# Row scale of a norm as a diagonal in the products that turn x, block inverses' last copies on ScalarE, and other places for the late modulation

## The chip, the cores and the metric

The kernel runs on one core of one Trainium2 chip. The metric is the device time of one execution in microseconds (us). The engines are named as the profile names them: PE is TensorE (PEld its weight loads), DVE is VectorE, ACT is ScalarE, SP is the engine whose queue issues nearly all DMAs. SBUF is the memory on the chip, PSUM the accumulators that PE writes, in banks of 128 rows by 512 f32.

## What is computed

One block of three sublayers on x of 256 rows (tokens) by 2048 columns, all in float32. Each sublayer has the same frame around its inner function:

```python
def sandwich_sublayer(x, fn, gain_pre, gain_post, shift, scale, gate, weight):
    h = modulate(rms_norm(x, gain_pre), shift, scale)   # h*(1+scale)+shift
    y = rms_norm(fn(h), gain_post)
    return x + weight * (1 + gate[:, None, :]) * y
```

The inner functions are a SwiGLU of width 5632 (`(silu(h @ w_gate) * (h @ w_up)) @ w_down`), a mixer, and a second SwiGLU. The mixer multiplies h by w_in (2048 x 5472), sends 512 columns through causal averages over 2, 4, 8 and 16 rows and four 128 x 128 products, and 24 heads of 64 through an RWKV-7 recurrence, and multiplies the joined result by w_out (2048 x 2048). Shift, scale and gate of the three sublayers, nine vectors of 2048, come from one product, `silu(c) @ w_ada + b_ada`, with a w_ada of 2048 x 18432 for a single row c. This product is called the modulation below; its vectors are numbered 0 to 8, and 6 and 7 are shift and scale of the third sublayer.

## The kernel before, in words

**Arithmetic.** A weight is loaded as f32 (`load`, L173, 1 MB as a rule, tile raw), and split into a rounded part hi (ACT, L185) and the rest lo (DVE, L186). The activations stand in hT, with the 2048 columns on the partitions in 16 blocks of 128, again as a high and a low part. Each product is three matmuls, hi with high, hi with low, lo with high (L201 and the wide form, L212 and L213).

**Norm and turn (`pre_begin` L389, `pre_rows` L399, `pre_block` L404).** The scale of a row is computed from the sum of its squares (`pre_begin`, or `post_rows` for the second and third sublayer). `pre_rows` multiplies x by it on ACT and writes y (L402). `pre_block` takes blocks of columns, in sizes of 2, 2, 4, 4 and 4: PE transposes y, 128 x 128 at a time, two columns by two halves of the rows into one bank (L417); ACT copies a column's 256 rows to the high part of hT with the norm's gain and the modulation (L421), copies it once more in full (L425; in the first block of the second and third sublayer column 1 is done on DVE instead, L423), and DVE subtracts for the low part (L426).

**Outer stage (`outer`, L631).** The first products of each sublayer run block by block behind these turned blocks. In an FFN the blocks of 2 and 2 are merged for most of the loads; the first block has two loads, and the merged second one ten. At fixed loads a `tick` runs one step of the modulation.

**Modulation.** `ada_step` (L259) does a quarter of the 2048 rows of w_ada for up to 1024 columns: DMAs into ada tiles (four in an FFN, two in the mixer), a multiply-add on DVE for each (L255, L257), and after four steps a product with ones on PE that sums over the partitions (`ada_mod`, L311) and an add of b_ada (L323). In the mixer the generator `ada_run` (L273) does the same through four places in x, which is copied out to memory meanwhile (L878) and back (L954); three loads run ahead of the sums. `ADA_AHEAD` lets it go as far as the third of the five blocks of vectors 6 and 7. The other two blocks are made in FFN2's outer stage, four steps beside the merged block (`TICKS2`, loads 3, 5, 7, 9) and four beside the next.

**The mixer's stages (`stage`, L882).** After its outer stage the mixer runs seven stages of 12 slots. Six have a part `rwkv_a` of the next pair of heads, with `rwkv_b` of the one before, and two pieces of weight products in each slot (w_in's, in the sixth also w_out's). The last has `rwkv_b` alone and three pieces in two slots. In here PE's order is fixed by hand (`self.ordered`): every matmul depends on the one listed before it. DVE's modulation sums are held behind the last operation marked urgent (`later`, `mark`). `rwkv_b` inverts lower triangular blocks in PSUM and SBUF by quarters: slot 4 multiplies into bank pb and copies it to pm, half on ACT (L1254), half on DVE (L1255), slot 5 multiplies pm with Z1 into bank zb and copies it into X, half on ACT (L1260), half on DVE (L1261), whose other entries DVE has filled by a mask (L1246). L1089 holds products of a decay tile with a constant triangle, plain f32 of 128 x 128, four in each of the six groups; L1118 uses bank ga in slot 4 of `rwkv_a`, L1234 copies At.

**w_out.** Two of its four column blocks are gathered in the stages (`out_piece`, L913), the other two run afterwards (L973, `rows_block` L596), the third in banks pb and zb, the fourth in sb, y and mm. Behind each column block follow statistics and z = y times gain (`post_rows`, L469), and behind the fourth the row scales and the update of x, which lead over to FFN2 (L541 to L557). L907 and L908 cast the finished rows of the recurrence into hT; the last of these wait for the recurrence's end.

The order on every engine and in SP's queue is laid out when the program is built, by priorities in the order of the code and a model of durations, within these dependences.

## Time and profile before

| | |
|---|---|
| median of 3 runs | 2139.73 us (2135.27 to 2146.23) |
| profiled execution | 2141.48 us |
| its span | 2139.7 us |
| mean granted clock of PE | 0.982 |

The span goes from the first to the last instruction in the profile. Its stages, read from the timeline (us from the start of the span):

| stretch | what runs |
|---|---|
| 0 to 27 | loads of x, first modulation, first row scales |
| 27 to 230 | FFN1's outer stage |
| 230 to 803 | rest of FFN1 |
| 803 to 875 | the mixer's outer stage |
| 875 to 1252 | six stages of the mixer |
| 1252 to 1306 | its last stage |
| 1306 to 1363 | third and fourth column block of w_out, and the hand-over |
| 1363 to 1565 | FFN2's outer stage; the merged block goes from 1372 to 1433 |
| 1565 to 2140 | rest of FFN2 |

How to read the rows. In the timeline a row has its start, its length, the engine, the line of the code, the operation, output <- input, the shape and a count of merged instructions; in brackets stands the idle time of the engine before it and who ended it. The table by stretches has for each the length, the busy time of PE, PEld, DVE, ACT and POOL with the number of instructions, PE's granted clock (1.00 is full, 0.50 half), the share of the DMA engines and GB/s. A row of a group has the count, then busy time in all, the mean ns of one, and idle time before. Matmuls are pipelined: a mean is longer than the pace, so paces are worked out from rows of several. Tile names are those of the program without numbers; "consts" are constants such as the identity.

### The profile page before, as it was taken

Reading aid. Unit: us, or ns where it says so; the run is one execution under the profiler, and the core shown is the slowest. Engines: PE = TensorE matmul, PEld = TensorE weight load, DVE = VectorE, ACT = ScalarE, POOL = GpSimd, SP = SyncE. Lnnn points to the kernel's source line nnn. Section 1 sums busy time; section 2 is a strip of 40 time slices with the busy share of each in tenths; the row PEclk is TensorE's granted clock in tenths of the full one; section 3 lists DMA queues with packets and bytes.
Section 4 is the critical chain, followed back from the end, with each engine's and each line's share of the span. In section 5 each row is a group of like instructions: output and inputs, shape, how many; then the busy total and the mean of one; then the engine's idle time right before and its main releaser. Section 6 shows DMA issues by size and latency. Waiting matters only on the chain.

```text
span 2139.7 us, 38742 instructions
## 1 busy us (share of the span) xinstructions
PE 2050.5 (96%) x15987; PEld 1826.6 (85%) x15987; DVE 1596.0 (75%) x2209; ACT 1023.4 (48%) x1502; POOL 0.2 (0%) x4
## 2 busy tenths in 40 slices
PE   3999999999999998999999999999999999999998
PEld 3999988888888887988888877899998888888886
DVE  6798898888887775778889865777898455555556
ACT  3544543444434556645445544643454344443453
POOL 0000000000000000000000000000000000000000
PEclk8999999999999999999999999999999999999999
DMA  9989879999888836655556434687986565555553
GB/s 310 359 310 319 288 274 327 330 321 318 313 320 297 285 119 205 182 179 163 162 164 191 147 124 138 238 314 272 328 289 235 193 196 187 187 188 192 191 193 123
DMA packets 315759, 506.62 MB, mean 237 GB/s; under 512 B 13013, under 2 KB 173886, under 8 KB 315070
## 3 DMA queue, kind: packets, MB, share of 16 engines
q1 hardware_dynamic: 314092, 500.78, 69.1%
q10 hardware_dynamic: 1490, 3.36, 0.4%
q8 instruction: 125, 2.05, 0.4%
q14 instruction: 52, 0.43, 0.1%
HBM read 499.87 MB, written 4.22 MB: 236 GB/s over the span
## 4 chain that ended last, share of the span: by engine, by line
PE 87%; DVE 6%; ACT 2%; DMA 2%; issue 2%; SPq 0%; DVEq 0%; ACTq 0%
PE mm L201 51%; PE mm L212 17%; PE mm L213 8%; PE zb L201 2%; PE sa L201 2%; PE ga L201 2%; DVE lo L186 2%; PE sb L201 2%; PE pb L201 2%; DVE acc L257 1%; DMA raw<-in_w_in_dram 1%; PE y L201 1%; ACT hi L185 1%; DMA ada<-in_w_ada_dram 0%; DVE act L668 0%
## 5 line engine op out<-in xcount | busy, mean ns | idle before, releaser
L185 ACT CAST hi<-raw 128x1024 fp32r<-128x1024 f32 (+2 forms) x766 | 695.5, 913 | 849.1 <-PE mm L201 532.8
L186 DVE TENSOR_TENSOR lo<-raw,hi 128x1024 fp32r<-128x1024 f32 (+2 forms) x766 | 798.2, 1050 | 393.1 <-ACT hi L185 389.4
L201 PE MATMUL mm<-hT,hi 128*128 128x256 f32 x3648 | 675.6, 287 | 11.9 <-DVE hT L426 4.4
L201 PEld LDWEIGHTS mm<-hT,hi 128*128 128x128 f32 x3648 | 571.1, 192 | 29.2 <-issue 7.2
L212 PE MATMUL mm<-hT,hi 128*128 128x512 f32 x1536 | 539.8, 395 | 0.0
L201 PE MATMUL mm<-hT,lo 128*128 128x256 f32 x1824 | 514.3, 283 | 1.5 <-DVE lo L186 1.5
L213 PE MATMUL mm<-hT,lo 128*128 128x256 f32 x1536 | 431.6, 281 | 0.0
L201 PE MATMUL mm<-hi,act 128*128 128x512 f32 (+1 forms) x1312 | 398.6, 384 | 0.0
L201 PEld LDWEIGHTS mm<-hT,lo 128*128 128x128 f32 x1824 | 349.4, 192 | 2.1 <-DVE lo L186 2.1
L257 DVE SCALAR_TENSOR_TENSOR acc<-ada,csilu,acc 128x1024 f32<-128x1024 f32 (+1 forms) x247 | 300.3, 1216 | 65.0 <-DMA ada<-in_w_ada_dram 62.9
L212 PEld LDWEIGHTS mm<-hT,hi 128*128 128x128 f32 x1536 | 288.8, 188 | 67.8
L213 PEld LDWEIGHTS mm<-hT,lo 128*128 128x128 f32 x1536 | 288.0, 187 | 0.2
L201 PEld LDWEIGHTS mm<-hi,act 128*128 128x128 f32 x1312 | 244.3, 188 | 48.7
L201 PE MATMUL mm<-lo,act 128*128 128x512 f32 (+1 forms) x656 | 251.8, 384 | 0.0
L201 PEld LDWEIGHTS mm<-lo,act 128*128 128x128 f32 x656 | 123.3, 188 | 24.3
L668 DVE TENSOR_TENSOR act<-act,mm 128x512 f32<-128x512 f32 x96 | 64.2, 679 | 2.3 <-PE mm L201 2.0
L257 DVE SCALAR_TENSOR_TENSOR ada<-x,csilu,ada 128x512 f32<-128x512 f32 (+1 forms) x45 | 41.5, 922 | 0.2
L201 PE MATMUL mm<-hi,work 128*128 128x512 f32 x128 | 40.8, 389 | 0.0
L201 PE MATMUL mm<-ones,acc 128*128 128x1 f32 x96 | 14.6, 281 | 26.1 <-DVE acc L257 26.1
L201 PEld LDWEIGHTS mm<-ones,acc 128*128 128x128 f32 x96 | 14.4, 236 | 26.9 <-DVE acc L257 21.4
L666 ACT COPY act<-mm 128x512 f32<-128x512 f32 x32 | 18.7, 585 | 34.2 <-PE mm L201 34.2
L201 PE MATMUL mm<-hi,hT 128*128 128x512 f32 (+1 forms) x88 | 30.9, 407 | 4.0 <-ACT hT L907 4.0
(374 smaller groups left out, 1686.1 us busy)
## 6 DMA issues: line engine op xcount, KB each, us to landing
raw<-in_ffn_w_down_dram SPq DMA_DIRECT2D x88, 1024.0 KB, 5.3
raw<-in_ffn_w_gate_dram SPq DMA_DIRECT2D x86, 1024.0 KB, 7.4
raw<-in_ffn_w_up_dram SPq DMA_DIRECT2D x86, 1024.0 KB, 5.3
ada<-in_w_ada_dram SPq DMA_DIRECT2D x152, 512.0 KB, 7.2
ada<-in_w_ada_dram SPq DMA_DIRECT2D x192, 256.0 KB, 5.3
raw<-in_w_in_dram SPq DMA_DIRECT2D x34, 1024.0 KB, 6.4
x<-in_w_ada_dram SPq DMA_DIRECT2D x64, 256.0 KB, 3.1
raw<-in_w_out_dram SPq DMA_DIRECT2D x16, 1024.0 KB, 5.2
```

What stands on the lines that cost most here:

```text
L185: a = nc.scalar.copy(hi, raw)
L186: d = nc.vector.tensor_tensor(lo, raw, hi.bitcast(F32), ALU.subtract)
L201: return self.pe(self.nc.tensor.matmul(ps, a, b, start=start, stop=stop))
L212: nc.tensor.matmul(ps.rearrange("p a t -> p (a t)"), hi, x.rearrange("p a t -> p (a t)"), start=start, stop=False)
L213: nc.tensor.matmul(ps[:, 0, :], lo, x[:, 0, :], start=False, stop=stop)
L257: self.later(nc.vector.scalar_tensor_tensor(acc, raw[:, i], ck, acc, ALU.mult, ALU.add))
L666: nc.scalar.copy(part, bank)
L668: nc.vector.tensor_tensor(part, part, bank, ALU.add)
```

## The change

- The row scales become two diagonal 128 x 128 tiles (`pre_scale`, the identity times the scale, on ACT). `pre_block` multiplies x with them in plain f32 products in place of transposing the scaled rows; `pre_rows` is gone with its 30 calls.
- In the whole of the mixer's outer stage the second copy of an odd column is made on DVE, not in its first block alone.
- In the block inverses both halves of pm and both halves of X are copied on ACT; the fill of X by the mask stands behind the copies of pm, and the last copies are no longer marked urgent.
- The modulation in the mixer has listed slots: seven of twelve in the six stages (before: four of five), slots 0 to 8 in the last. Its products with ones go to slots 1, 8, 10, 11, in the last stage to 2 to 5, with bank sb there. What is left runs in slot 9 of the last stage, and x comes back behind it.
- The last pieces of w_out's first two column blocks alternate by twos.
- Beside the third column block of w_out one step of the modulation follows each of its four loads. In FFN2's outer stage the ticks beside the merged block are gone; those of the next block stay.
- The tile ones has one column; the warm-up products use another constant.

```diff
-TICKS2 = ((3, 5, 7, 9), (1, 3, 5, 7))
+TICKS2 = (1, 3, 5, 7)
-ADA_FFN1, ADA_MIXER, ADA_FFN2 = 2.8, 0.8, 12
-SLOTS, A_SLOTS, MOD_SLOTS = 12, (0, 2, 4, 5, 6, 7, 9), (1, 3, 8, 10, 11)
+ADA_FFN1, ADA_FFN2 = 2.8, 12
+SLOTS, A_SLOTS = 12, (0, 2, 4, 5, 6, 7, 9)
+ADA_SLOTS, MOD_SLOTS = ((0, 1, 2, 7, 8, 10, 11), range(9)), ((1, 8, 10, 11), (2, 3, 4, 5))
...
-        self.ones = self.tile(const, [P, P], tag="ones")
+        self.ones = self.tile(const, [P, 1], tag="ones")
...
-            self.nc.tensor.matmul(ps, self.ones, self.consts[:, :512], start=True, stop=True)
+            self.nc.tensor.matmul(ps, self.blocks, self.consts[:, :512], start=True, stop=True)
...
-                self.ada_mod(cols, self.acc, sums, self.bank("ga"))
+                self.ada_mod(cols, self.acc, sums, self.bank(self.mod_bank))
...
-    def pre_rows(self, tt, k0, n):
-        cs = slice(k0 * P, (k0 + n) * P)
-        return self.nc.scalar.activation(self.y[:, tt, cs], self.x[:, tt, cs], AF.Copy, scale=self.rpre[tt])
+    def pre_scale(self, tt):
+        if tt == 0:
+            self.scale = self.tile(self.small, [P, 2, P], tag="scale", bufs=1)
+        return self.nc.scalar.activation(self.scale[:, tt, :], self.ident, AF.Copy, scale=self.rpre[tt])
...
-                    nc.tensor.transpose(ps[:, j, tt * P:(tt + 1) * P], self.y[:, tt, k * P:(k + 1) * P], self.ident)
+                    self.mul(ps[:, j, tt * P:(tt + 1) * P], self.x[:, tt, k * P:(k + 1) * P], self.scale[:, tt, :])
...
-                if gates and k == 1:
+                if (gates or s == 1) and k % 2:
                     nc.vector.tensor_scalar(t[:, i + j, :], ps[:, j, :], g, sh, ALU.mult, ALU.add)
...
                 self.later(self.post_update(tt, k0, n))
-                self.pre_rows(tt, k0, n)
...
-            act += [self.pre_rows(0, 0, 2)]
+            act += [self.pre_scale(0)]
...
-            act += [self.pre_rows(1, 0, 2)]
+            act += [self.pre_scale(1)]
...
-                slots += 1
-                if a and int(slots * ADA_MIXER) > parts and (s in MOD_SLOTS or not ends):
-                    parts += 1
+                if s in ADA_SLOTS[not a] and (s in MOD_SLOTS[not a] or not ends):
                     ends = next(ada, None)
...
-            for q, kc in ((0, 1), (0, 2), (1, 1), (1, 2), (0, 0), (1, 0), (0, 3), (1, 3)):
+            for q, kc in ((0, 1), (0, 2), (1, 1), (1, 2), (0, 0), (1, 0)):
                 yield from out_piece(q, kc)
+            two = [out_piece(q, 3) for q in range(2)]
+            for q in (0, 0, 1, 1, 0, 0, 1, 1):
+                yield next(two[q])
...
-        for _ in ada:
-            pass
-        nc.sync.dma_start(flat_x, dram)
+        self.mod_bank = "sb"
+        def back():
+            for _ in ada:
+                pass
+            nc.sync.dma_start(flat_x, dram)
...
-        stage(None, b, b_old, pieces, 1.5, {0: lambda: late(0, 1), 1: lambda: late(2, 3, 12, 13), 4: gain})
+        stage(None, b, b_old, pieces, 1.5, {0: lambda: late(0, 1), 1: lambda: late(2, 3, 12, 13), 4: gain, 9: back})
...
             def load(kc):
-                return self.load(I["w_out"], 4 * kc, 4, q * 512, 512)
+                raw = self.load(I["w_out"], 4 * kc, 4, q * 512, 512)
+                if q == 2:
+                    self.ada_step(self.mm)
+                return raw
...
-        X = self.tile(self.w2p, [P, U, C], tag="X", bufs=1)
-        nc.vector.tensor_tensor(X.rearrange("p u (a t) -> p u a t", a=2), Z1.unsqueeze(2).broadcast_to([P, U, 2, H]),
-                                self.hmask.unsqueeze(1).unsqueeze(3).broadcast_to([P, U, 2, H]), ALU.mult)
...
-        nc.scalar.copy(pm[dn[0]], ps[dn[0]])
-        nc.vector.tensor_copy(pm[dn[1]], ps[dn[1]])
+        for h in range(2):
+            nc.scalar.copy(pm[dn[h]], ps[dn[h]])
+        X = self.tile(self.w2p, [P, U, C], tag="X", bufs=1)
+        nc.vector.tensor_tensor(X.rearrange("p u (a t) -> p u a t", a=2), Z1.unsqueeze(2).broadcast_to([P, U, 2, H]),
+                                self.hmask.unsqueeze(1).unsqueeze(3).broadcast_to([P, U, 2, H]), ALU.mult)
...
-        nc.scalar.copy(X[up[0], :, H:], ps[up[0]])
-        self.mark(nc.vector.tensor_copy(X[up[1], :, H:], ps[up[1]]))
+        for h in range(2):
+            nc.scalar.copy(X[up[h], :, H:], ps[up[h]])
...
-                if q and i in TICKS2[q > 1] and self.ada_pos < self.ada_end[(7, 6)]:
+                if q == 2 and i in TICKS2:
                     self.ada_step(mm)
```

Beside these, `begin` calls `pre_scale` for both halves after `pre_begin`, and the calls of `pre_rows` in the blocks of FFN1 and in `next_block` are gone.

More of the change, by code (lines that the diff above doesn't have):

```diff
@@ L316, in ada_mod @@
             for i in range(2 * n):
-                self.mul(ps[:, i:i + 1], acc[:, i // n, i % n * P:(i % n + 1) * P], self.ones[:, :1])
+                self.mul(ps[:, i:i + 1], acc[:, i // n, i % n * P:(i % n + 1) * P], self.ones)
         else:
@@ L872, in mixer @@
                 take(which, i, banks[2 + which][:, i, :])
-        self.ordered = True
+        self.ordered, self.mod_bank = True, "ga"
         dram = self.tile(self.dram, [P, 2 * D], tag="x", bufs=1)
@@ L879, in mixer @@
         ada = self.ada_run(ADA_AHEAD, [flat_x[:, i * 4 * T:(i + 1) * 4 * T] for i in range(4)])
-        slots = parts = ends = 0
+        ends = None
         def stage(a, b, b_old, pieces, rate, tasks={}):
-            nonlocal slots, parts, ends
+            nonlocal ends
             for s in range(SLOTS):
@@ L1358, in begin @@
             self.pre_begin(tt)
+            self.pre_scale(tt)
     def begin_rest(self, mm):
@@ L1395, in block @@
                 self.ada_finish(((1, 0), q), mm)
-                for tt in range(2):
-                    self.pre_rows(tt, k0, n)
                 self.pre_block(0, k0, n, mm)
```

## The prediction

> **What bounds the kernel.** I read the page first, then the list of what TensorE (PE) waits for, the timeline of PE, and the busy time by stretches.
>
> ```profile
> span 2139.7 us, 38742 instructions
> ...
> PE 2050.5 (96%) x15987; PEld 1826.6 (85%) x15987; DVE 1596.0 (75%) x2209; ACT 1023.4 (48%) x1502; POOL 0.2 (0%) x4
> ...
> PE 87%; DVE 6%; ACT 2%; DMA 2%; issue 2%; SPq 0%; DVEq 0%; ACTq 0%
> ```
>
> PE is busy for 96% of the span and carries 87% of the chain that ended last. So a change pays by taking out one of PE's waits, or a stretch at a lower clock, and costs by giving PE more instructions. Of the waits, two lines belong to this change (total, times, longest):
>
> ```profile
> PE mm L201 <- DVE acc L257: 26.1, 4, 14.2
> PE zb L201 <- DVE pm L1255: 7.8, 4, 2.5
> ```
>
> The timeline places these and other waits. In brackets stands the idle time ahead of the instruction and who ended it:
>
> ```profile
> 822.82 0.47 PE L417 MATMUL mm<-consts,y 128*128 128x128 f32 x1 [1.69 <-ACT G L425]
> 824.64 0.48 PE L417 MATMUL mm<-consts,y 128*128 128x128 f32 x1 [1.35 <-ACT G L425]
> 833.34 0.50 PE L201 MATMUL sa<-hT,hi 128*128 128x256 f32 x2 [2.52 <-ACT hi L185]
> 1086.46 0.69 PE L201 MATMUL zb<-Z,pm 32*32 32x32 f32 x32 [2.53 <-DVE pm L1255]
> 1213.09 1.10 PE L201 MATMUL ga<-t,consts 128*128 128x512 f32 x2 [2.85 <-DVE mod L323]
> 1305.53 0.80 PE L201 MATMUL mm<-hi,hT 128*128 128x512 f32 x1 [4.01 <-ACT hT L907]
> 1422.14 2.54 PE L201 MATMUL mm<-ones,acc 128*128 128x1 f32 x16 [2.35 <-DVE acc L257]
> 1480.49 2.83 PE L201 MATMUL mm<-ones,acc 128*128 128x1 f32 x16 [2.86 <-DVE acc L257]
> ```
>
> After some of them PE runs at half clock (the column PEclk, ahead of the DMA share, the last but one), after others not. The rows are also needed for the load of VectorE (DVE, the third busy time):
>
> ```profile
> 822.00:829.00 7.00, 4.80 (x19) 4.10 (x20) 2.98 (x6) 4.22 (x9) 0.00 (x0) 0.54 0.91 292
> 1086.00:1092.00 6.00, 5.54 (x96) 5.27 (x98) 4.86 (x10) 1.60 (x3) 0.00 (x0) 1.00 0.95 246
> 1195.00:1260.00 65.00, 62.15 (x910) 52.63 (x909) 55.18 (x129) 34.35 (x70) 0.00 (x0) 1.00 0.40 135
> 1260.00:1307.00 47.00, 40.96 (x523) 31.40 (x522) 22.05 (x41) 16.15 (x29) 0.00 (x0) 0.93 0.39 132
> 1307.00:1375.00 68.00, 64.47 (x336) 52.76 (x334) 47.45 (x110) 41.94 (x94) 0.00 (x0) 0.97 0.48 162
> 1375.00:1415.00 40.00, 39.69 (x336) 39.69 (x337) 32.97 (x32) 24.33 (x33) 0.00 (x0) 0.96 1.02 369
> 1425.00:1430.00 5.00, 5.00 (x25) 5.00 (x25) 2.36 (x3) 0.16 (x1) 0.00 (x0) 0.50 0.98 345
> 1484.00:1488.00 4.00, 4.00 (x20) 4.00 (x20) 1.93 (x3) 0.00 (x0) 0.00 (x0) 0.50 0.27 36
> ```
>
> The wait of 2.53 us at 1086 was followed by a clock of 1.00, that of 2.35 at 1422 by at least 5 us at 0.50, that of 2.86 at 1480 by at least 4 us at 0.50. I count 2.5 and 2.0 us of lost PE time there, besides the waits: 4.9 us for each.
>
> **1. Diagonal products instead of scaled rows.** Three norms, 16 columns of 128, two halves of the rows: 96 transposes of y become 96 f32 products of x with a diagonal. The trace has both kinds, the f32 product as L1089's (24 products that appear as 48 matmuls):
>
> ```profile
> L417 PE MATMUL mm<-consts,y x96: 270/273/476, 27.3 to 1562.4; 128*128 128x128 f32 x96
> ...
> 105.03 1.07 PE L417 MATMUL mm<-consts,y 128*128 128x128 f32 x8
> 106.32 0.74 PE L201 MATMUL mm<-hT,hi 128*128 128x256 f32 x4 [0.22 <-ACT hT L421]
> 107.76 0.39 PE L201 MATMUL mm<-hT,hi 128*128 128x256 f32 x1 [0.71 <-DVE hT L426]
> 1134.75 1.16 PE L201 MATMUL sa<-consts,bk 128*128 128x128 f32 x8
> L201 PE MATMUL sa<-consts,bk 128*128 128x128 f32 x48 | 6.8, 286 | 0.0
> L402 ACT ACTIVATE y<-x,row 128x512 f32<-128x512 f32 x18 | 12.2, 729 | 0.0
> L423 DVE TENSOR_SCALAR G<-mm,gs,mod x1: 544/544/544, 805.8 to 805.8; 128x256 f32<-128x256 f32 x1
> ```
>
> Eight transposes take 1.07 us; less the 0.27 of one alone (the median), a seventh is 0.114 us each. Eight matmuls, which are four products, take 1.16; by the same working (mean 0.286) one takes 0.124 and a product 0.249. So a product is 0.135 us longer, and all 96 cost 13.0 us at full clock if nothing hides them. Part is hidden. In a block of four columns, eight transposes fill two banks, and PE then waits 0.22 us for the copy hT and 0.71 us for its low part. That chain starts when the first bank is full, which is now 4 x 0.135 = 0.54 us later; the second bank's extra falls into the waits. So a block of four in the two FFNs costs 0.54, six of them 3.2. In the mixer PE is interleaved and no wait covers it: three blocks at 1.08, 3.2. Blocks of two columns have one bank: 0.54 each; of the six I leave out the very first, behind which PE waits for acc again (26.1 us less 14.2, 2.35 and 2.86 leaves 6.7 for that wait): 2.7. Sum **+9.1** (3 if more is hidden; over 13 only where blocks meet half clock).
>
> The Trainium skill speaks against this edit: "TensorE: Matmul & The Clock Gate", section Terms, says that the transpose mode is four times faster for FP32. By that a product would cost 0.456 us and the term, worked out in the same way, 23.3; an estimate. The rows above show 2.2 times, so the sum goes by them.
>
> In exchange ScalarE (ACT) loses the scalings L402, 18 wide ones (12.2 us) and 12 narrow ones, against six diagonals, and PE reads x straight after DVE's update, without ACT between. Over most of the span ACT is no bound, and I count nothing for it. In the mixer's first stretch it matters: the waits at 822.82, 824.64 and 833.34 (5.6 us) end with ACT, which copies the blocks one after another, and the clock of 0.54 over 822 to 829 took 4.80 x 0.46 = 2.2 us more. There ACT also loses the seven odd second copies, which go to DVE at 0.54 us each; DVE has 2.98 of the 7 us in that row. I take **-6.0** (0 to -7.8).
>
> **2. The last copies of the block inverses on ACT.** The 2.53 us at 1086 come from DVE's queue, not from the data:
>
> ```profile
> 1078.81 0.36 ACT L1254 COPY pm<-pb 32x256 f32<-32x256 f32 x1
> 1085.17 0.68 DVE L1246 TENSOR_TENSOR X<-Z,consts 128x512 f32<-128x512 f32 x1
> 1085.88 0.43 DVE L1255 COPY pm<-pb 32x256 f32<-32x256 f32 x1
> L257 DVE SCALAR_TENSOR_TENSOR acc<-ada,csilu,acc 128x1024 f32<-128x1024 f32 x217 | 277.7, 1280 | 60.8 <-DMA ada<-in_w_ada_dram 59.4
> ```
>
> ACT copied its half of pm at 1078.81; DVE reached the other half at 1085.88, behind modulation sums, splits and X. With both halves on ACT the second follows about 0.36 us after the first, some 6 us earlier. All four waits in the list go: **-7.8**. Behind the two new copies ACT's hi split is queued, 0.7 us later, of which PE has pieces in hand; DVE's Z1, which the next product reads too, comes ahead of X. The X copies become serial on ACT and wait for DVE's mask product, now placed behind pm; DVE is eased there, so I count nothing. If DVE's next step is late instead, the term goes to 0.
>
> **3. Modulation in other slots.** Counted through the slots, the generator ended in slot 3 of the sixth stage; with seven slots of twelve it leaves seven sums for the last stage, and its last product comes in slot 9 there, three slots after them. The wait at 1213.09 (L323 holds bank ga) goes with its slot, but the block that moves to slot 1 of the fourth stage meets the same bank's next use in slot 2: half, -1.4. The sixth stage gains six sums of 1.28 us: DVE 55.18 + 7.7 less 0.85 for the two copies is 62.0 of 65 us. That is nearly full, **+1.5** (0 to 4, three sums ahead of urgent steps). Both together **+0.1**. The last stage has DVE 22.05 of 47; its seven sums (9 us) fit, but may stand before a step of the serial chain: **+0.5** (-2 to +4). The copy of x back, now in slot 9, still lies ahead of its first reader, the row statistics behind the stage. The shorter ones tile and the other operand of the warm-up leave the counts as they are.
>
> The interleaved last pieces bring nothing. The wait of 4.01 us at 1305.53 is for the casts of the last rows, and the pieces that could fill it already run ahead of it:
>
> ```profile
> 1299.77 0.59 PE L201 MATMUL sa<-hi,hT 128*128 128x512 f32 x1
> ```
>
> **4. A block of modulation beside w_out.** Four steps (16 sums, 20.5 us of DVE, 32 loads of 256 KB, 8.4 MB) leave FFN2's merged block and go beside the third column block of w_out. In FFN2 they filled the DMA engines (share 1.02 in 1375 to 1415) and ended in the wait of 1422: **-4.9**. The following block keeps its four steps and the wait at 1480, but starts without a backlog: half, **-2.4** (0 to -4.9).
>
> Beside w_out DVE has 47.45 + 20.5 = 67.9 of 68 us, though part of the sums can start in the stage before. There the ada tiles are two, not four, and the loads share SP's queue with w_out's:
>
> ```profile
> 1303.04 12.43 SPq L175 DMA_DIRECT2D raw<-in_w_out_dram  x2
> 1321.12 16.75 SPq L175 DMA_DIRECT2D raw<-in_w_out_dram  x4
> ...
> 991.54 0.37 SPq L247 DMA_DIRECT2D x<-in_w_ada_dram  x1
> 992.36 0.34 SPq L1037 DMA_DIRECT2D lg<-in_g_dram  x1
> 993.22 0.57 SPq L247 DMA_DIRECT2D x<-in_w_ada_dram  x1
> ...
> ada<-in_w_ada_dram SPq DMA_DIRECT2D x192, 256.0 KB, 5.3
> x<-in_w_ada_dram SPq DMA_DIRECT2D x64, 256.0 KB, 3.1
> ```
>
> Two tiles at a time take a landing (3.1 to 5.3 us) and two sums (2.56): 5.7 to 7.9 us. From 1303 to the third column block's neighbour (about 1327, the second of the four from 1321.12) there are three steps, six such turns: 34 to 47 us for 24, with one load's pieces, 5.5 us by the pace of those four, in hand. In the code's order that is a stall of 5 to 18 us. But the queue isn't laid out in the code's order: 991.54 and 993.22 are the two halves of one modulation load (all others come in pairs), next to each other in the code, and a gate load stands between. A load that waits for a tile lets others pass. So I take the nearest row, FFN2's wait of 2.35 for the same four steps: **+2.0** (0 to 18).
>
> **The sum.** 9.1 - 6.0 - 7.8 + 0.1 + 0.5 - 4.9 - 2.4 + 2.0 = -9.4 us, from the profiled execution's 2141.5 (span 2139.7) to 2132.1. The median of the runs is 1.8 lower, 2139.7, so 2130.3.
>
> **Rivals.** (a) w_out gives back what FFN2 gains: 8 us there and the wait at 1480 stays. For it: DVE's 67.9 of 68. Against it: slack from the last stage. -9.4 + 6.0 + 2.4 = -1.0: 2138.7. (b) Everything goes well: 1480's wait and the mixer's go wholly, w_out and the sixth stage cost nothing, and one more us of products is hidden: -18.1, 2121.6. (c) A wait takes the place of those at 1086: with PE 2.5 us earlier, the next mask or split on DVE is late, and only a third is gained: -4.2, 2135.5. (d) Slower: SP's queue keeps the code's order beside w_out, with a landing of 5.3 us; PE stalls 18 us there instead of 2: +6.6, 2146.3. It decides from the turn at which six take longer than the 24 + 5.5 us, 4.9 us. (e) The products take four times a transpose: the term is 14.2 more, +4.8, 2144.5. In a sentence by itself: this is what the Trainium skill's section Terms, named above, implies, and the trace's f32 rows speak against it.
>
> **Chances.** Forecast 0.37, (a) 0.22, (b) 0.20, (c) 0.10, (d) 0.08, (e) 0.03. A measurement of this kernel can tell about 0.5%, 10.7 us, so faster means below 2129.0. That is (b), and the forecast's lower half with w_out at 0 or FFN2 whole, with a little of (c): 0.42. Slower means above 2150.4, reached by (d) with half clock after each stall, or (d) and (e) with further waits: 0.06. The rest, 0.52, is the same. The range leaves out a tenth on each side: 2117 (beyond (b)) to 2144 (short of (d)). The likeliest case's own range, with its terms between neighbouring bounds, is 2125 to 2136.
>
> **What would show it.** Right: L417's group gone, 192 f32 matmuls with x as weights, about 24 us busy, and the blocks' first hT copy about 0.5 us later; no waits at 822 to 833; "PE zb <- DVE pm" gone and nothing in its place; 1422's wait gone, FFN2's merged block at full clock. Wrong: PE waits for DMA raw or acc beside w_out, a long SP wait on DVE acc ahead of w_out loads, waits of PE for DVE in the sixth stage, or products that pace at 0.45 us.

## The result, and the profile after

After the change the median is 2130.07 us (8 runs, 2125.57 to 2132.83), before it 2140.55 (8 runs, 2135.27 to 2146.23). The ratio is 0.9946 with a 95% interval of 0.9929 to 0.9962: by the medians 10.5 us less, and the interval leaves out no change. The forecast was 2130.3, and the 2129.0 from which it would have called the kernel faster is not reached. It came out right as a sum, but two of its terms were wrong by more than the whole change, in opposite directions. The sections below show which.

The profiled execution took 2132.83 us. Its page, the lines that answer to those of before:

```profile
span 2131.0 us, 38906 instructions
...
PE 2051.9 (96%) x16083; PEld 1829.5 (86%) x16083; DVE 1591.6 (75%) x2204; ACT 1010.5 (47%) x1483; POOL 0.2 (0%) x4
...
PE 81%; DVE 4%; DMA 4%; ACT 1%; issue 1%; SPq 0%; DVEq 0%; ACTq 0%
```

PE's share of the chain that ended last fell from 87% to 81%: a wait that was not there before now lies on it. In the list of what PE waits for, the line "PE zb <- DVE pm" is gone as forecast, but the wait for acc has not shrunk from 26.1 us:

```profile
PE mm L202 <- DVE acc L258: 33.3, 3, 15.0
...
PE mm L202 <- DVE hT L428: 7.2, 9, 5.1
```

The timeline of PE after, at the places of the forecast's rows and some others (line numbers are up to 8 higher in the mixer):

```profile
106.84 2.03 PE L202 MATMUL mm<-scale,x 128*128 128x128 f32 x16
167.98 2.03 PE L202 MATMUL mm<-scale,x 128*128 128x128 f32 x16
229.12 2.03 PE L202 MATMUL mm<-scale,x 128*128 128x128 f32 x16
808.20 0.38 PE L202 MATMUL sa<-hT,hi 128*128 128x256 f32 x1 [0.66 <-ACT hT L423]
898.55 0.37 PE L202 MATMUL ga<-ar,bk 64*128 64x128 f32 x1 [0.91 <-DVE ar L1117]
923.06 0.75 PE L202 MATMUL pb<-Z,T 32*32 32x32 f32 x64
1073.80 0.69 PE L202 MATMUL zb<-Z,pm 32*32 32x32 f32 x32
1192.76 1.13 PE L202 MATMUL ga<-t,consts 128*128 128x512 f32 x2
1288.01 0.79 PE L202 MATMUL mm<-hi,hT 128*128 128x512 f32 x1 [6.70 <-ACT hT L906]
1335.11 3.58 PE L202 MATMUL mm<-ones,acc 128*128 128x1 f32 x16 [11.17 <-DVE acc L258]
1366.19 0.50 PE L202 MATMUL mm<-hT,hi 128*128 128x256 f32 x2 [1.71 <-ACT hT L423]
1434.36 0.58 PE L202 MATMUL mm<-hT,hi 128*128 128x256 f32 x1 [5.07 <-DVE hT L428]
1475.38 1.84 PE L202 MATMUL mm<-ones,acc 128*128 128x1 f32 x16
1553.24 1.95 PE L202 MATMUL mm<-scale,x 128*128 128x128 f32 x16
```

- 106.84 to 229.12: a block of four columns in FFN1, sixteen matmuls now, 61.14 us apart.
- 923.06, 1073.80 and 1192.76 follow without a wait. Before, PE waited 2.53 us at the second of these places and 2.85 at the third, and at the first, which the prediction had not listed, 3.20 us (the other rows are for the table below):

```profile
804.49 0.38 PE L201 MATMUL sa<-hT,hi 128*128 128x256 f32 x1 [0.66 <-ACT hT L421]
897.88 0.37 PE L201 MATMUL ga<-ar,bk 64*128 64x128 f32 x1 [0.91 <-DVE ar L1109]
925.75 1.08 PE L201 MATMUL pb<-Z,T 32*32 32x32 f32 x64 [3.20 <-DVE Z L1185]
1365.24 0.51 PE L201 MATMUL mm<-hT,hi 128*128 128x256 f32 x2 [1.16 <-ACT hi L185]
1561.60 1.03 PE L417 MATMUL mm<-consts,y 128*128 128x128 f32 x8
```

- 1335.11: a new wait of 11.17 us beside w_out, and the product with ones behind it runs at half clock: 3.58 us, with 0.50 granted from 1335.00 to 1338.50, against 1.84 at 1475.38, with 1.00 granted. The wait at 1288.01 was 4.01.
- 1475.38 without a wait: the product that is left in FFN2 no longer stops PE; the other one is the row at 1335.11. At 1434.36 it waits 5.07 us for a low part hT, which stands on DVE behind a sum for the late modulation (1432.69), and that sum waits 2.32 us for its load.

These rows cut both spans into places. Of each place its length in us, worked out from the starts (of before, 1305.53 stands in the prediction; FFN2's last block is 1561.60 and 1553.24):

| place | before | after | difference |
|---|---|---|---|
| to the mixer's first product with hT | 804.49 | 808.20 | +3.7 |
| the mixer's outer stage, to the first ga<-ar,bk | 93.39 | 90.35 | -3.0 |
| the stages, to the end of the wait for the last cast | 407.65 | 389.46 | -18.2 |
| w_out, to FFN2's first product | 59.71 | 78.18 | +18.5 |
| FFN2's outer stage, to its last block | 196.36 | 187.05 | -9.3 |
| the rest | 578.10 | 577.76 | -0.3 |

The first row says little. Over thirteen profiles of these two kernels and the versions below, whose FFN1 differs in part 1 alone, this place comes at 803.04 to 809.24: on average at 805.9 in the five with transposes there and at 806.7 in the eight with products.

The forecast had -7.2 for the stages (its copies, slots and last stage) and +2.0 for w_out. They are off by 11 and by 16.5 us. The question of the experiments is what made these two.

### The profile page after: what moved, and what is told of

Its sections match the earlier page's. It is cut to its first block, busy times and chain, and to the rows that moved or that the text cites. A ratio compares the mean times of both kernels' runs of the same rounds, so it can differ in the third digit from the quotient of the medians.

```text
span 2131.0 us, 38906 instructions
## 1 busy us (share of the span) xinstructions
PE 2051.9 (96%) x16083; PEld 1829.5 (86%) x16083; DVE 1591.6 (75%) x2204; ACT 1010.5 (47%) x1483; POOL 0.2 (0%) x4
## 4 chain that ended last, share of the span: by engine, by line
PE 81%; DVE 4%; DMA 4%; ACT 1%; issue 1%; SPq 0%; DVEq 0%; ACTq 0%
PE mm L202 47%; PE mm L213 16%; PE mm L214 8%; PE ga L202 2%; PE sb L202 2%; PE sa L202 2%; DMA ada<-in_w_ada_dram 2%; DVE lo L187 1%; PE zb L202 1%; PE pb L202 1%; DMA raw<-in_w_out_dram 1%; PE y L202 1%; DVE acc L258 1%; DMA raw<-in_w_in_dram 1%; ACT hi L186 1%
## 5 line engine op out<-in xcount | busy, mean ns | idle before, releaser
L423 ACT ACTIVATE hT<-mm,mod,gs 128x256 fp32r<-128x256 f32 x48 | 27.1, 570 | 12.6 <-PE mm L202 12.6
```

Source lines behind the costliest of these rows:

```text
L423: a = nc.scalar.activation(self.hT[:, k, 0, :], ps[:, j, :], AF.Identity, scale=g, bias=sh)
```

## Experiments

Each kernel was timed against the kernel before on its own chip, so versions are compared by the ratio; their profiles are compared by place.

**The parts alone.** Part 1 alone: `pre_scale`, the products and the odd copies put into the kernel before. Part 2 alone:

```diff
-        nc.vector.tensor_copy(pm[dn[1]], ps[dn[1]])
+        nc.scalar.copy(pm[dn[1]], ps[dn[1]])
...
-        self.mark(nc.vector.tensor_copy(X[up[1], :, H:], ps[up[1]]))
+        nc.scalar.copy(X[up[1], :, H:], ps[up[1]])
```

and the mask product behind pm's copies. Part 3 alone: `ADA_SLOTS`, `MOD_SLOTS`, the bank and `back`. And the kernel after without part 4, the block beside w_out:

```diff
-                if q == 2:
-                    self.ada_step(self.mm)
...
-TICKS2 = (1, 3, 5, 7)
+TICKS2 = ((3, 5, 7, 9), (1, 3, 5, 7))
```

> The kernel before with part 1 alone: diagonal products in place of the scalings and transposes, odd second copies of the mixer's first stage on DVE. The trace of after places this part's price: the FFN1 outer stage ends 3.3 us later than before (228.5 to 231.8), the mixer starts 3.7 us later, and the mixer's outer stage gives 3.0 us back (its waits of 1.69, 1.35 and 2.52 us are gone). Theory (price by place): the same positions here, then about 2 to 3 us more in FFN2's six blocks, so a profile 2 to 4 us longer than before's, 2142 to 2145. Rival 1 (the prediction's terms, +9.1 and -6.0): +3.1 as well, but with 4 to 5 us lost in FFN1's blocks and 6 won in the mixer. Rival 2 (the products are free, what FFN1 lost came from other parts): 0 to -3. A median ratio between 1.000 and 1.002 fits the theory.

Measured: 2145.40 us, ratio 1.0018 (0.9999 to 1.0036), +3.9 us. The size fits both the theory and the prediction's terms, the places neither. In the profile the mixer's outer stage takes 91.46 us instead of 93.39, and FFN2's outer stage 195.76 instead of 196.36, where the theory had 2 to 3 us more. Another 4.4 us lie in the mixer's stages, which part 1 does not touch (325.66 us from the first ga<-t,consts to the sixth, before 321.25): there the same waits for pm are followed by a lower clock than before. The last section has the rows.

> The kernel before with part 2 alone: both halves of the block inverses' last two copies on ACT. Theory (prediction's term): the four waits of PE for DVE pm go (0.45, 2.53, 2.53 and 2.26 us), nothing takes their place, the third to fifth stage's pitch falls from 62.4, 65.2 and 65.2 us by 0.5 to 2.6 each, the first wait (3.20 us at 925.75 for DVE Z) and the one at 1213 (2.85 us, DVE mod) stay: -7.8, about 2132 to 2134. Rival (the stages' gain in the trace of after, 21 us, is mostly this part: an eased DVE also ends the waits at 925 and 1213): -13 to -18, 2123 to 2128. Rival 2 (DVE's next step is late in its place): 0 to -3.

Measured: 2138.75 us, ratio 0.9989 (0.9969 to 1.0009), -2.4 us, no difference that can be told. All four waits for pm are gone, and three new ones stand 1 to 2 us behind their places:

```profile
1022.47 0.37 PE L201 MATMUL ga<-ar,bk 64*128 64x128 f32 x1 [1.96 <-DVE bv L1120]
1088.57 0.37 PE L201 MATMUL ga<-ar,bk 64*128 64x128 f32 x1 [1.96 <-DVE bv L1120]
1152.89 0.58 PE L201 MATMUL ga<-ar,bk 64*128 64x128 f32 x1 [1.69 <-DVE bv L1120]
```

On DVE, ahead of the first of these:

```profile
1018.17 0.75 DVE L257 SCALAR_TENSOR_TENSOR ada<-x,csilu,ada 128x512 f32<-128x512 f32 x1
1019.66 0.75 DVE L257 SCALAR_TENSOR_TENSOR ada<-x,csilu,ada 128x512 f32<-128x512 f32 x1
1021.13 0.68 DVE L1254 TENSOR_TENSOR X<-Z,consts 128x512 f32<-128x512 f32 x1
1021.73 0.68 DVE L1120 TENSOR_TENSOR bv<-ga,v 128x512 f32<-128x512 f32 x1
```

DVE's queue was late, and pm was only the first in it that PE needed. bv (L1120), which reads bank ga and so holds up PE's next product into that bank, stands behind the same sums and X. The edit also takes away a mark that holds sums back, but that did not let these in: before, two sums stand ahead of X at the same place (1017.04 and 1018.53). Between the profiles the stages are no shorter: 409.86 us against 407.65. The second rival holds.

> The kernel before with the modulation's slots alone: seven chosen slots of twelve instead of 9.6, products in other slots, the rest of the sums in the last stage, the copy of x back in slot 9. Theory (where the traces put the gain): fewer sums of 1.28 us per stage take DVE out of the way of the inverse's Z, so the wait of 3.20 us at 925.75 and the half clock behind it go (the first pitch 59.3 to about 53), and the wait at 1213 goes (2.85 and little else): -8 to -11 in the stages, pm's waits stay about as they are or shrink, the last stage loses 0 to 1: 2129 to 2133. Rival (the prediction's term): +0.6, 2141 to 2142, with the stage's pitches unchanged.

Measured: 2123.13 us, ratio 0.9916 (0.9889 to 0.9942), -18 us: more than the theory had, where the prediction had +0.6. The waits at 925 and 1213 are gone, and also those for pm, though half of pm is copied on DVE here as before:

```profile
955.38 0.69 PE L202 MATMUL zb<-Z,pm 32*32 32x32 f32 x32 [0.46 <-DVE pm L1257]
```

0.46 us is left of each of the four; this is the first. The pitch from stage to stage, by the starts of ga<-t,consts (of after, 1192.76 above is the sixth):

| us | first | second | third | fourth | fifth | sum |
|---|---|---|---|---|---|---|
| before | 59.32 | 62.37 | 65.16 | 65.17 | 69.23 | 321.25 |
| slots alone | 51.83 | 62.37 | 63.10 | 62.21 | 63.10 | 302.61 |
| after | 51.82 | 61.80 | 62.51 | 61.61 | 62.51 | 300.25 |

So the slots make 18.6 of the 21.0 us that the stages gained. In the first pitch one sees how. Before, three sums stand on DVE ahead of Z's transpose, for which PE waits; after, two, and Z is done 4.4 us earlier, though the stage began 0.7 us later:

```profile
904.58 1.27 DVE L257 SCALAR_TENSOR_TENSOR acc<-x,csilu,acc 128x1024 f32<-128x1024 f32 x1
912.71 1.27 DVE L257 SCALAR_TENSOR_TENSOR acc<-x,csilu,acc 128x1024 f32<-128x1024 f32 x1
915.12 1.27 DVE L257 SCALAR_TENSOR_TENSOR acc<-x,csilu,acc 128x1024 f32<-128x1024 f32 x1
925.26 0.43 DVE L1185 STREAM_TRANSPOSE Z<-Z 128x256 f32<-128x256 f32 x1
```

```profile
911.58 1.27 DVE L258 SCALAR_TENSOR_TENSOR acc<-x,csilu,acc 128x1024 f32<-128x1024 f32 x1
913.38 1.27 DVE L258 SCALAR_TENSOR_TENSOR acc<-x,csilu,acc 128x1024 f32<-128x1024 f32 x1
920.86 0.44 DVE L1193 STREAM_TRANSPOSE Z<-Z 128x256 f32<-128x256 f32 x1
```

> The kernel after without the third block beside w_out: its four steps back in FFN2's merged block, as before. In the traces the stretch from the late casts' wait to FFN2's first product grew from 59.7 to 78.2 us, and FFN2's outer stage fell from 199.4 to 189.7. Theory (the block beside w_out costs more than it gains): the 11.17 us wait beside w_out and its half clock go, the wait for ACT hT at 1288 falls from 6.7 towards 4 us (sums of this block stood ahead of the last serial steps on DVE), and FFN2 gets its waits for acc back: -18 to -21 and +10, so 8 to 11 us shorter than after, a profile of about 2121 to 2124. Rival (the move pays for itself, as the prediction had it: +2.0 against -4.9 and -2.4): 5 us longer than after, about 2138. Rival 2: no difference, 2131 to 2134.

Measured: 2118.14 us, ratio 0.9890 (0.9866 to 0.9914), apart from the 0.9946 of after: without the block the kernel is 12 us faster. w_out takes 59.24 us, as before the change, FFN2's outer stage 195.25, and the last cast's wait is 4.31 us instead of 6.70. The theory holds, the prediction's account of part 4 doesn't.

**Which slots, or how many.** The slots alone once more, seven of twelve too, but spread evenly, and the products in before's slots:

```diff
-                if s in ADA_SLOTS[not a] and (s in MOD_SLOTS[not a] or not ends):
+                slots += 1
+                due = int(slots * 7 / 12) > parts if a else s in ADA_SLOTS[1]
+                if due and (s in MOD_SLOTS[not a] or not ends):
+                    parts += 1
```

> The slots alone again (which took the kernel before from 2142.5 to 2123.1), with the same seven sums in twelve slots, but spread evenly (slots 1, 3, 5, 6, 8, 10, 11) instead of the chosen 0, 1, 2, 7, 8, 10, 11, and products in before's slots. Theory (placement: the sums in slots 3 to 6 stood ahead of the inverse's Z and in 10 and 11 ahead of pm): the wait of 3 us for DVE Z at 925 stays, and part of the waits for pm; 2130 to 2140. Rival (the rate, 7 in place of 9.6 a stage, is what counts): the same as with the chosen slots, 2121 to 2126, no wait above 1 us in the stages.

Measured: 2141.29 us, ratio 0.9983 (0.9970 to 0.9996). Nearly all of the gain is gone, so the places count, as the theory said: those of the sums and those of the products together, since the edit moves both. One thing it had wrong: the wait at 925 did not come back, so there the lower rate is enough. The first pitch is 51.93 us; then the waits are as long as ever:

```profile
952.33 1.07 PE L202 MATMUL zb<-Z,pm 32*32 32x32 f32 x32 [2.27 <-DVE pm L1261]
1019.36 0.69 PE L202 MATMUL zb<-Z,pm 32*32 32x32 f32 x32 [2.33 <-DVE pm L1261]
1081.83 2.05 PE L202 MATMUL ga<-t,consts 128*128 128x512 f32 x2 [3.44 <-DVE mod L324]
```

**Why w_out became 18.5 us longer.** On SP, ACT and DVE beside w_out in the kernel after:

```profile
1319.38 2.60 SPq L248 DMA_DIRECT2D ada<-in_w_ada_dram  x4
1322.38 0.38 SPq L176 DMA_DIRECT2D raw<-in_w_out_dram  x1
1325.63 0.81 SPq L248 DMA_DIRECT2D ada<-in_w_ada_dram  x2
```

```profile
1330.70 0.62 ACT L186 CAST r<-raw 128x512 fp32r<-128x512 f32 x1 [3.68 <-DMA raw<-in_w_out_dram]
```

```profile
1326.18 1.28 DVE L258 SCALAR_TENSOR_TENSOR acc<-ada,csilu,acc 128x1024 f32<-128x1024 f32 x1
1331.35 0.69 DVE L187 TENSOR_TENSOR k<-raw,r 128x512 fp32r<-128x512 f32 x1 [2.39 <-ACT r L186]
1333.17 0.69 DVE L187 TENSOR_TENSOR bv<-raw,v 128x512 fp32r<-128x512 f32 x1
1333.77 1.28 DVE L258 SCALAR_TENSOR_TENSOR acc<-ada,csilu,acc 128x1024 f32<-128x1024 f32 x1
```

PE stops at 1323.9 (1335.11 less the wait) at the product with ones and waits for the block's last sum. That sum stands on DVE behind splits of w_out's next tile, and this tile, issued at 1322.38 right behind four modulation loads, is first used at 1330.70. So two things are late, the product and the tile. To tell them apart, all sums and loads stay, and only the product is moved, to FFN2's second block:

```diff
+        if k0 == KD - 4 and psum is None:
+            self.held_mod = lambda mm: self.ada_mod(cols, self.acc, None, self.tile(mm, [P, 512], tag="mm"))
...
+                if k0 == 2:
+                    self.held_mod(mm)
                 self.ada_finish(((7, 6), [b[0] for b in FIRST_BLOCKS].index(k0)), mm)
```

> The kernel after, the block's four steps still beside w_out, but its last product (16 small matmuls that wait for acc, 11.17 us in after) is emitted ahead of FFN2's second block instead of in the middle of w_out. Theory A (the stall is the product's place in PE's queue): the wait and the 3.6 us of the product at half clock go and nothing follows, 14 to 16 us less than after: a median of 2114 to 2117, as fast as without the block. Theory B (the weights are late as well): in after the next w_out tile was issued at 1322.38 behind modulation loads and its first split ran only at 1330.70, so PE waits for that split instead, from about 1325 to 1331, at most 5 to 7 us are gained, median 2123 to 2126. Rival C (sums and loads, not the order, fill the stretch): 0 to 2, 2128 to 2131.

Measured: 2117.71 us, ratio 0.9870 (0.9855 to 0.9885), 16 us less than after. Theory A has the size; by place 12.5 us of it are here. The stretch falls from 78.18 to 65.63 us; of the 6 us left above the 59.2 without the block, 2.67 are theory B's. PE waits for a split, and ACT has just waited 3.42 us for the tile:

```profile
1332.62 0.67 PE L202 MATMUL sb<-hi,hT 128*128 128x512 f32 x1 [2.67 <-ACT hi L186]
```

```profile
1331.95 2.18 ACT L186 CAST hi<-raw 128x512 fp32r<-128x512 f32 x4 [3.42 <-DMA raw<-in_w_out_dram]
```

What the product held up can be seen too. The fourth column block has three accumulators, sb, y and mm. In after its products into sb and y run ahead of the product with ones, those into mm, from weight tiles already split, all behind it; with the product held back they begin beside the others. The first of them in after and in this run:

```profile
1338.54 0.56 PE L202 MATMUL mm<-hi,hT 128*128 128x256 f32 x1
```

```profile
1315.32 0.28 PE L202 MATMUL mm<-hi,hT 128*128 128x256 f32 x1
```

The accumulator mm and the product's own tile come from the same pool of two. Whether this pool or the order on PE alone put them there, the runs don't separate.

**Half of the block beside w_out.**

```diff
-                if q == 2:
+                if q == 2 and kc < 2:
                     self.ada_step(self.mm)
...
-                if q == 2 and i in TICKS2:
+                if q and i in ((3, 7), TICKS2)[q > 1] and self.ada_pos < self.ada_end[(7, 6)]:
```

> The kernel after, but only two of the block's four steps beside w_out, the other two (with the product) beside FFN2's second block. Theory (the cost beside w_out is the queue: loads between w_out's tiles, and a product that waits): with half the loads and no product, the stretch from the late casts to FFN2's first product falls from 78 us to 60 to 63, and FFN2's merged block keeps its gain (no wait for acc at 1400): a median of 2111 to 2117, at or below the kernel without the block (2118). Rival (each step beside w_out costs its share): half of the 12 us between after and the kernel without the block, 2123 to 2126. Rival 2 (FFN2's waits come back whole): 2117 to 2121.

Measured: 2112.30 us, ratio 0.9849 (0.9836 to 0.9862). The theory holds: w_out takes 59.49 us, and FFN2's outer stage 182.93, less than after's 187.05, with no wait for acc in it. By the ratios this version is 21 us faster than the kernel after and 32 faster than before.

**Products in the mixer alone**, on the kernel without the block:

```diff
+                    if s == 1:
                         self.mul(ps[:, j, tt * P:(tt + 1) * P], self.x[:, tt, k * P:(k + 1) * P], self.scale[:, tt, :])
+                    else:
+                        nc.tensor.transpose(ps[:, j, tt * P:(tt + 1) * P], self.y[:, tt, k * P:(k + 1) * P], self.ident)
```

The FFNs have `pre_rows` back as well.

> The kernel after without the block beside w_out (2118.1), with diagonal products in the mixer's norm alone: the two FFNs have their scalings and transposes back. Theory (by the positions with part 1 alone: FFN1's outer stage 1.5 to 3 us, FFN2 0.6 us later, the mixer 2 us earlier): 2 to 4 us less, median 2113 to 2117. The prediction's prices for the FFNs (0.54 for each block, 2.2 in FFN1 and 2.7 in FFN2) give 4 to 5, 2113 to 2114. Rival (in the FFNs the products are hidden, and ACT's relief is worth something there too): 0 to +3, 2118 to 2121.

Measured: 2122.35 us, ratio 0.9896 (0.9883 to 0.9910), against 0.9890 (0.9866 to 0.9914) without that edit. That is the rival's size, but the intervals are too wide to shut out the theory's -2 to -4. The blocks of FFN1 gain their half us each, and it can't be seen in the time. The largest difference between the two profiles is in FFN2's last part, 528.2 us against 525.5 from 1539.63 and 1536.85 to the gain's transpose, where no block lies.

**On the version with half of the block.** Three edits, timed together. Part 2 taken back is its diff above, reversed. The other two, each product issued twice and the two steps at the later tiles:

```diff
-                    self.mul(ps[:, j, tt * P:(tt + 1) * P], self.x[:, tt, k * P:(k + 1) * P], self.scale[:, tt, :])
+                    for _ in range(2):
+                        self.mul(ps[:, j, tt * P:(tt + 1) * P], self.x[:, tt, k * P:(k + 1) * P], self.scale[:, tt, :])
```

```diff
-                if q == 2 and kc < 2:
+                if q == 2 and kc > 1:
```

> The version with two steps beside w_out (2112.3, ratio 0.985) without part 2: the inverse's last copies are split between ACT and DVE again, as before. Theory (the chosen slots alone emptied DVE's queue ahead of pm: with the slots alone its four waits were 0.46 us each): +1.5 to +2, a ratio of 0.985 to 0.987. Rival (the prediction's term: the copies are worth the four waits of 7.8 us): +7 to +8, a ratio of 0.988 to 0.989 and waits above 2 us for DVE pm.

Measured: 2114.86 us, ratio 0.9887 (0.9870 to 0.9903); against the version with the later tiles below, timed beside it, +3.2 us by the medians and 4.7 by the ratios. The waits for pm are 0.46 us, four times, and the five pitches add up to 302.6 us against 300.3, as the theory had it. It left out what comes behind them: from the sixth ga<-t,consts to the last cast the profile has 97.78 us against 95.28. So the copies are worth nearly 5 us here, between the theory's 2 and the rival's 7 to 8. The rival's waits of over 2 us are not there; what makes the 2.5 us behind the pitches is not shown.

> The version with two steps beside w_out, with each of the 96 diagonal products issued twice into the same place: 96 x 0.249 = 23.9 us more of PE's work in the blocks' heads. Theory (the prediction's way of costing them: in an FFN block of four only the first bank's share lands, in the mixer nothing hides it): 1.0 us a block in the FFNs (ten blocks less one that is hidden behind acc: 9), 2.0 for the mixer's three blocks of four and 1.0 for its two of two (8), in all about +13 to +17, a ratio of 0.991 to 0.993. Rival 1 (all of it lands): +24, 0.996. Rival 2 (it is mostly hidden, so that the +9.1 was too high): +3 to +7, 0.986 to 0.988.

Measured: 2123.37 us, ratio 0.9922 (0.9909 to 0.9936), +11.7 us against the version with the later tiles. By place FFN1's outer stage is 3.3 us longer and FFN2's 3.1, less than the 9 costed for both, and the mixer's outer stage is 92.06 against 93.19, where 8 was costed: there the doubled products are hidden. That is some 5 us where the products are, rival 2's size. In the rest of FFN1, up to the mixer's first product with hT, the profile is another 9 us longer, though only the mixer's first block has products there, and the others differ by up to 7. This stays unexplained, and the total proves little. The row for one block:

```profile
106.79 3.82 PE L202 MATMUL mm<-scale,x 128*128 128x128 f32 x32
```

> The version with two steps beside w_out, with the steps at the third and fourth of the block's weight tiles instead of the first and second, so that their sums can't run ahead into the last stage. Theory (the wait of 6.70 us for the last late cast was 4.3 without the block's sums, which stood on DVE ahead of the last serial steps): that wait falls to 4.0 to 4.4 us and nothing is late next: -2 to -3, a ratio of 0.983 to 0.984. Rival (later loads now stand between the last w_out tiles or their sums ahead of its splits): a wait of 2 us or more beside w_out or at FFN2's start, 0.985 to 0.988.

Measured: 2111.63 us, ratio 0.9865 (0.9851 to 0.9879), the same as with the first two tiles (0.9849). The wait stayed 6.70 us: my edit did not do what I thought. Three sums still ran ahead of the last serial steps, two in the first row here and one in the second:

```profile
1280.44 2.60 DVE L258 SCALAR_TENSOR_TENSOR acc<-ada,csilu,acc 128x1024 f32<-128x1024 f32 x2
1286.59 1.28 DVE L258 SCALAR_TENSOR_TENSOR acc<-ada,csilu,acc 128x1024 f32<-128x1024 f32 x1
```

Naming a later tile had not moved the work: the block's first loads were issued at 1268.98, with the first two tiles at 1269.39, and the first two multiply-adds ran at 1280.44 and 1280.86. So an order was given. The last serial product (d, which makes yT) is marked urgent, which holds sums back:

```diff
+        if g == NP // 2 - 1:
+            self.mark(d)
```

> The version with two steps beside w_out, in which the block's sums are ordered on DVE behind the last stage's last serial step (the product that makes y for the late casts). Moving the steps to later weight tiles had left the wait of 6.70 us as it was: three sums still ran at the same place, two ahead of t and one ahead of y. Theory (these sums are the difference between the 6.70 us and the 4.31 without the block): the wait falls to 4.0 to 4.4 us, and the sums have room later: -2 to -3 us against the same version without the order, a ratio of 0.983 to 0.985. Rival (the sums then meet w_out's splits, or the loads behind them come late): the wait falls, but w_out's stretch grows from 59.5 by 2 us or more, no gain.

Measured: 2110.79 us, ratio 0.9843 (0.9824 to 0.9863). The wait:

```profile
1286.69 0.50 PE L202 MATMUL mm<-hi,hT 128*128 128x512 f32 x1 [4.31 <-ACT hT L906]
```

4.31 us as without the block, so those sums were the difference. w_out then takes 60.88 us instead of 59.49, and no gain in time can be told. This last version has the lowest median of all, though not apart from the one with half of the block.

## Why the prediction was right, and where it was not

**The diagonal products** (+9.1 and -6.0, net +3.1): the +3.9 (-0.2 to +7.7) alone fits the sum, but its interval reaches zero, and by place the two terms are both too large. A product is (2.03 - 1.07) / 8 = 0.12 us longer than a transpose by the rows of a block of four (1.07 is before's 105.03 row), forecast 0.135. A block of four in FFN1 costs 0.5 us (61.14 against 60.63 with transposes, from 164.62 to 225.25 in the profile of the slots alone; before itself has 60.63 and 61.57), forecast 0.54. In FFN2 the last block's distance is 59.12 against 59.17: nothing, where 0.54 a block stood. In the mixer "no wait covers it" was wrong: with twice the products its outer stage takes 92.06 us, and with single ones 90.35 to 93.19 in nine profiles, 91.7 on average. The four profiles with transposes average 93.4. So the change is worth 1.7 us there, as much as 4.3 for the products less the 6.0 of relief, but with a cost of about nothing and a relief of about 2. The transposes' rule of the Trainium skill, "TensorE: Matmul & The Clock Gate", section Terms (transpose mode four times faster for FP32), is not borne out: sixteen products take 3.82 us in the doubled version against 2.03 for eight, 0.224 each, and a transpose 1.07 / 8 = 0.134, 1.7 times by this working and 2.2 by the forecast's.

**The inverse's copies** (-7.8): wrong in size. The waits went, but alone the next one in DVE's queue took their place. That is rival (c)'s mechanism; its size, a third, can't be checked on -2.4 us (-6.6 to +1.9). With the slots, which empty that queue, the copies are worth 0.6 us in each of four pitches, and nearly 5 us in all where they were taken back from the version with half of the block.

**The slots** (+0.1, and +0.5 for the last stage): this is the step that failed most, -18 us instead. The working counted how many sums each stage gets and where the product goes. It did not ask which serial step stands behind each sum on DVE. Yet the part on the copies had said it: DVE reached pm "behind modulation sums, splits and X". I charged that wait to the copies, though part 3 moves those sums, and the wait of 3.20 us at 925.75, of the same kind, is in no term.

**Beside w_out** (+2.0, -4.9, -2.4): FFN2 gained 9.3 us, a little more than the 7.3 forecast, but w_out lost 18.5. The failed sentence is "So I take the nearest row, FFN2's wait of 2.35 for the same four steps". The working just above it had a stall of 5 to 18 us, from two tiles at a time; it was thrown out since loads may pass each other on SP. They do: in after, w_out's tile of 1322.38 is issued ahead of the block's last two loads (1325.63), which the code has before it. But the product with ones stood on PE ahead of work whose weights were ready, and its last sum stood behind the splits of a late tile. The run with the product held back prices that at 12.5 us of the stretch and leaves 6 for late tiles and the clock. The 2.4 us at the last cast come on top: the last stage was forecast with -2 to +4 for its own seven sums, and the block's first sums were not among them.

So -18 where +0.6 stood, -2.4 where -7.8 stood, and +12 where -5.3 stood: errors of 18.6, 5.4 and 17 us that cancel within what the runs leave uncertain. The range held the time, but the sum was luck. The parts measured singly (+3.9, -2.4, -18, +12) add up to -4.5, not -10.5, with 4 to 6 us of uncertainty each, so they don't show how the parts act on each other. The table by place adds up to the two profiles' difference.

## What to carry to other kernels

Here the waits belonged to the queue ahead of the late operation more than to that operation: before moving one to another engine, look at what else in the same queue is due next, and price the edit that shortens the queue first. When a piece of background work is moved, follow it into every queue whose order is fixed, to its last instruction. Here the loads could pass each other, but one small product in PE's queue cost more than all the rest of the move. And when a sum of terms comes out right, check it by place.

## What the runs showed of the chip that was not expected

Whether PE's clock falls behind a wait does not go by the wait's length alone. Before, the wait of 2.53 us at 1086.46 was followed by a clock of 1.00 (the prediction shows the row). With part 1 alone, which changes nothing in these stages, the same wait was followed by half clock. The product, and the stretch behind it in the table by stretches (PE's clock is the column before the last two):

```profile
1088.65 1.06 PE L201 MATMUL zb<-Z,pm 32*32 32x32 f32 x32 [2.53 <-DVE pm L1255]
```

```profile
1089.70:1093.00 3.30, 3.30 (x23) 3.08 (x23) 2.63 (x6) 0.36 (x1) 0.00 (x0) 0.50 1.02 251
```

Nor does the first product tell. In the evenly spread version it takes 1.07 us behind the wait of 2.27 at 952.33 and 0.69 behind that of 2.33 at 1019.36, but there too the clock is 0.56 from 1020.10 to 1024.00. So the prediction's price for the waits for pm, which counted no slow clock behind them, held for the profile that it read and not for every run of these stages. What decides is not shown.
